# Wide tiles with rows of 2048 instead of 2112 bytes, and every pool 64 bytes further up

## The chip, the cores and the metric

The kernel runs on one core of a Trainium2 chip. TensorE (PE) multiplies matrices, VectorE (DVE) and ScalarE (ACT) work element by element, GpSimd (POOL) does small things and issues some of the transfers, SyncE (SP) issues the others. The engines run side by side and wait for each other by semaphores. Operands lie in SBUF, the core's own memory of 128 partitions; an address here is a byte within a partition, the same in all 128. TensorE writes its results to PSUM, in banks of 512 float32 per partition. A matmul has two operands in SBUF: the stationary one, 128 columns that are loaded ahead of it, and the moving one, here 256 or 512 columns of 4 bytes that stream through.

The metric is device time in microseconds, from runs of the whole program.

## The reference

One layer on a sequence of 512 tokens with 1024 features, all in float32. Three blocks follow each other, each with a norm ahead and behind and a residual:

```python
h = swiglu(rmsnorm(x, norm_ffn1_pre[l]), w_ffn1_in[l], w_ffn1_out[l])
x = x + FFN_RESIDUAL_SCALE * rmsnorm(h, norm_ffn1_post[l])
h = mixer(rmsnorm(x, norm_mix_pre[l]), w_mix_in[l], conv_w[l], conv_b[l],
          gate_i_bias[l], gate_f_bias[l], mlstm_norm[l], w_mix_out[l])
x = x + rmsnorm(h, norm_mix_post[l])
h = swiglu(rmsnorm(x, norm_ffn2_pre[l]), w_ffn2_in[l], w_ffn2_out[l])
x = x + FFN_RESIDUAL_SCALE * rmsnorm(h, norm_ffn2_post[l])
```

`swiglu` multiplies by a matrix of 1024 x 5632, gates one half with the other and multiplies by one of 2816 x 1024. The mixer projects to 3088 columns, runs a short convolution over one half and a two-way recurrent head (mLSTM, in chunks of 128) over the other, and projects back. The weights, some 86 MB by their shapes, come from HBM.

## The kernel before

**How products are made.** A float32 product is made of three matmuls in the type float32r: each operand is split into a high part (ScalarE copies it into float32r) and a low part (VectorE subtracts the copy), and high x high, high x low and low x high are added up in PSUM. `split` does this. On top of it, most of the large products use a seven-product scheme for 2 x 2 blocks in place of eight. So VectorE and ScalarE prepare weights all the time while TensorE multiplies.

**The stages**, in order of the program, with the line of the matmuls in each:

- Feed-forward, first matrix: `plain` (L542) for the first columns and `mm_part` (L516) for the rest, 256 moving columns each. The stationary operand is a block of weights, the moving one is the flipped activation, 4 rows of 128 features to a wide tile.
- Feed-forward, second matrix: `product_out` (L723) and `mm_out` (L745), with 512 moving columns. Here the moving operand is the weights and the stationary one a block of 128 columns of the activation.
- Mixer: L950 projects the values (256 and 272 moving columns in turn), `mm_cols` (L507) and `seven` with `mm_part` (L516) the rest; small matmuls for the heads (L1277 to L1370); L1425 projects back, 512 moving columns.
- The second feed-forward block, as the first.

TensorE's order is that of the program in most places; a scheduler orders the other engines' work when the program is built. That order is the same before and after the change on all engines.

**Where tiles lie.** Pools lie one behind the other in a partition: small constants, then `xpool` (4 tiles of 4096 bytes), `big` (13 wide tiles), `wpool` (12 of 4096: the split weights `whi`, `wlo`, `ws`, `wt`), `rawp` (4 of 4096: weights as loaded), then `gbp`, `t4p`, `t2p` (4096, 4096 and 2048 bytes). In the built program `xpool` starts at byte 7872, which is 30 x 256 + 192. All sizes behind it are multiples of 256, so every tile there starts at 192 more than a multiple of 256. This text calls what an address has over a multiple of 256 its remainder.

A wide tile is made by `bigt()`: 4 rows of `BW = 528` float32, 2112 bytes each, 8448 in all (33 x 256). Most users take the first 512 columns of a row; only a few need 528 (the mixer's values and their weights have 16 more columns for gates). Since 2112 is 8 x 256 + 64, the four rows start at remainders 192, 0, 64 and 128.

This sets the remainders of the operands:

| matmul line | moving operand | stationary operand |
|---|---|---|
| L542, L516, L507 | rows of wide tiles: 192, 0, 64, 128 in turn | weights in `wpool`: 192 |
| L723 | weights in `wpool`: 192 | blocks of a wide tile used as one row of 2048 columns, or of `xpool`: 192 |
| L745 | weights in `wpool`: 192 | rows of wide tiles: all four |
| L1425 | weights in `wpool`, or a wide tile used as one row: 192 | rows of wide tiles: all four |
| L950 | rows of 2112 bytes: all four | rows of wide tiles: all four |

The inner loop of L516, with `x` a view of a wide tile, shows how rows change with each matmul:

```python
for ww, xx in ((hi, 0), (hi, 1), (lo, 0)):
    for k in range(4):
        pin(nc.tensor.matmul(
            o, ww[:, k, :], x[xx][:, k, :], start=first and n == 0, stop=n == 11, skip_group_check=True))
```

Of the kernel before, what the change touches and what calls it, by code (L numbers as in the profile page):

```python
# [8 lines left out]
F32 = mybir.dt.float32  # L9
F32R = mybir.dt.float32r  # L10
# [6 lines left out]
P = 128  # L17
# [19 lines left out]
BW = 528  # L37
# [4 lines left out]
def encoder_kernel(ctx: ExitStack, tc: tile.TileContext, a: dict, out: bass.AP):  # L42
    nc = tc.nc

    const = ctx.enter_context(tc.tile_pool(name="const", bufs=1))
    xpool = ctx.enter_context(tc.tile_pool(name="xpool", bufs=NT))
    big = ctx.enter_context(tc.tile_pool(name="big", bufs=13))
# [11 lines left out]
    def nm(s):  # L59
        uid[0] += 1  # L60
        return f"{s}_{uid[0]}"

    def bigt(dt=F32):
        return big.tile([P, 4, BW], dt, tag="big", name=nm("big"))

    def ps():
        return psum.tile([P, 512], F32, tag="ps", name=nm("ps"))
# [10 lines left out]
    def f32(ap):  # L78
        return ap.bitcast(F32)

    def blk(i, n=P):
        return slice(i * n, (i + 1) * n)

    def ch(v):
        return v.rearrange("p (c t) -> p c t", t=P)
# [211 lines left out]
    def w_get(ahead=2):  # L297
        w_split(max(0, 1 + ahead - len(ready)))
        return ready.pop(0)
# [62 lines left out]
    def split(hi, lo, src, eng=nc.vector):  # L362
        latest["hi"] = nc.scalar.copy(out=hi, in_=src)  # L363
        if pinned["act"]:
            pin(latest["hi"])
        latest["lo"] = eng.tensor_tensor(out=lo, in0=src, in1=f32(hi), op=ALU.subtract)  # L366
        pin(latest["lo"])
# [34 lines left out]
    def xq_tile(xq, key):  # L402
        if key not in xq["q"]:
            xq["q"][key] = bigt(F32R)
        return xq["q"][key]
# [7 lines left out]
    def flip_q(tb, xs, xq, halves=(0, 1), bank=None):  # L413

        full = []
        for b in halves:
            pt = bank or ps()
            for k in range(4):
                pin(nc.tensor.transpose(out=pt[:, blk(k)], in_=xs[:, blk(4 * b + k)], identity=ident))  # L419
            hi, lo = xq_hl(xq, (b, tb // 2))  # L420
            split(hi[:, :, blk(tb % 2)], lo[:, :, blk(tb % 2)], ch(pt))
            if b not in xq["f"]:
                xq["f"][b] = bigt()
            if bank:
                return lambda fn: pin(fn(xq["f"][b][:, :, blk(tb)], ch(pt)))
            full.append((b, pt))
        for b, pt in full:
            pin(nc.scalar.copy(xq["f"][b][:, :, blk(tb)], ch(pt)))
# [91 lines left out]
    def ffn(xq, between, finish, mid=None, within=None, ahead=(2, 2, 1, 1), late=None, prep=None, block=0):  # L520
# [4 lines left out]


        h = [bigt() for _ in range((NF + 3) // 4)]
        spare.extend(h[-1][:, q, 0:512] for q in (2, 3))

# [362 lines left out]
    def v_split():  # L892
        for i in range(4):
            if not loaded:
                w_load(1)
            (raw,), _ = loaded.pop(0)
            bt = bigt(F32R).rearrange("p q f -> p (q f)")
            hi, lo = (bt[:, blk(n, 2 * BW)].rearrange("p (k f) -> p k f", k=2) for n in range(2))
            split(hi[:, :, 0:512], lo[:, :, 0:512], raw.rearrange("p (k f) -> p k f", k=2))
            rg = rawg[:, 2 * i:2 * i + 2, :]  # L900
            nc.gpsimd.tensor_copy(out=hi[:, :, 512:BW], in_=rg)
            nc.gpsimd.tensor_tensor(out=lo[:, :, 512:BW], in0=rg, in1=f32(hi[:, :, 512:BW]), op=ALU.subtract)
            wv.append((hi, lo))
# [14 lines left out]
    def within1(tb):  # L918
        if tb >= 2:
# [6 lines left out]
            (2, 1): lambda: flip_q(2, st1[2], xT1), (3, 0): lambda: mark.update(latest), (3, 1): lambda: flip_q(3, st1[3], xT1),  # L926
        },
        finish1, wgates, within1, (1, 1, 1, 0), late1, v_split)
    xq = st["xq"]

# [1 line left out]
        return xq_hl(xq, (k // 4, tb // 2))[hl][:, k % 4, blk(tb % 2)]  # L932


    vaug = bigt()
    vv = vaug.rearrange("p c (h e) -> p c h e", e=BW // 4)
    nc.gpsimd.memset(vv[:, :, :, DV:DV + 1], 1.0)
    spread = t2()
# [26 lines left out]
    with tc.issue_after(mark["pow"].ins):  # L965
        RA, RB = bigt(), bigt()
        nc.gpsimd.memset(RA[0:36, 0:2], 0.0)
        I, F = RA[0:36, 0, 0:512], RA[0:36, 1, 0:512]
        T1, T2 = RA[0:36, 2, 0:512], RA[0:36, 3, 0:512]
        B, A = RB[0:36, 0, 0:512], RB[0:36, 1, 0:512]  # L970
        CM, U = RB[0:36, 2, 0:512], RB[0:36, 3, 0:512]
        nc.gpsimd.memset(U, 1.0)
        nc.gpsimd.memset(ch(U)[:, :, 0:1], 0.0)
        HLT = bigt(F32R)
        UHL, IHL = HLT[:, 0, 0:512], HLT[:, 1, 0:512]
        nc.gpsimd.memset(f32(HLT[:, 0:2]), 0.0)
        sel = HLT.rearrange("p q f -> p (q f)")[:, 2 * BW:2 * BW + 8 * P].rearrange("p (j m) -> p j m", m=P)
        QT = bigt()
        Q1, Q2 = QT[:, 0, 0:512], QT[0:36, 1, 0:512]
        nc.gpsimd.memset(QT[:, 0:2], 0.0)  # L980
        parl = QT[0:36, 2, 0:2 * DK]
        nc.gpsimd.tensor_copy(parl.rearrange("p (e x) -> p e x", x=DK), par.broadcast_to([36, 2, DK]))
        gm = const.tile([36, 4, 8], F32, name="gm")
        amax, gsum, mprev, aco = gm[:, 0, 0:4], gm[:, 1, 0:4], gm[:, 2, :], gm[:, 3, 0:4]
        nc.vector.memset(mprev[:, 0:1], NEG)
# [261 lines left out]
        pn2[:, 256:272], parl, acd.rearrange("p q c -> p (q c)"),  # L1247
        start=True, stop=True,
    )
    Ct = bigt()  # L1250
    Cf = Ct.rearrange("p q f -> p (q f)")
    Cs = Cf[:, 0:12 * 129].rearrange("p (q i e) -> p q i e", q=4, i=3)
    nat1 = Cf[:, 1552:2064].rearrange("p (c r) -> p c r", r=P)
# [147 lines left out]
    for n, k in enumerate(MIXK):  # L1401
        if n < 5:
            wmo[k] = w_get(0)
        else:
            raw = rawp.tile([P, 1024], F32, tag="raw", name=nm("raw"))
            nc.sync.dma_start(raw, wo[blk(k), :])
            bt = bigt(F32R).rearrange("p q f -> p (q f)")
            split(bt[:, 0:1024], bt[:, 1024:2048], raw)
            wmo[k] = (bt[:, 0:1024], bt[:, 1024:2048])
    for tb in range(NT):  # L1410
# [58 lines left out]
```

## Time and profile before

| | |
|---|---|
| median of 3 runs | 888.0 us (886.79 to 888.97) |
| the profiled execution | 888.25 us, span from first to last instruction 886.5 us |
| mean granted TensorE clock | 0.999 |
| TensorE busy | 99% of the span, 6039 matmuls |
| VectorE, ScalarE, GpSimd busy | 83%, 55%, 11% |
| DMA | 123.24 MB, 139 GB/s on average |

The page of a profile gives busy times of the engines, a picture of the span in slices, the DMA queues, the chain of work that ended last (followed back from the last instruction, step by step, to what released it), and the costliest groups of instructions. A group's row has the line, engine, operation, what is written and read (`ps<-big,whi`: the moving operand first, then the stationary one), the shape and the count; then busy time, the mean duration of one, and the idle time ahead of it with what ended it. The chain can also be had in order of time: start, length, and how many instructions of one line followed each other. Matmul durations are modelled and overlap, so a matmul's real cost is read from start to start.

### The profile page before, as it was taken

How to read it: one execution, taken by the hardware profiler on the slowest of the kernel's cores; microseconds unless marked ns; L12 is line 12 of the kernel's file. 1: busy time of each engine (PE TensorE's matmuls, PEld its weight loads, DVE VectorE, ACT ScalarE, POOL GpSimd, SP SyncE). 2: the span in 40 equal slices, each digit the busy share in tenths (PEclk: the TensorE clock that was granted, in tenths of full speed). 3: DMA queues.
4: the chain of work that ended last, by engine and by line, in shares of the span. 5: the costliest groups of instructions: out<-in, count | busy, mean ns of one | idle time of the engine just before them, and what ended most of it. 6: DMA issues, size and time to landing. Idle time of an engine off the chain costs nothing.

```text
span 886.5 us, 15403 instructions
## 1 busy us (share of the span) xinstructions
PE 875.6 (99%) x6039; PEld 807.4 (91%) x6039; DVE 731.8 (83%) x1159; ACT 491.8 (55%) x855; POOL 93.7 (11%) x123
## 2 busy tenths in 40 slices
PE   8999999999999999999999999999999999999997
PEld 6999999999988889988988888999999999988885
DVE  6989898988889978887588757898898988869956
ACT  7656455544656645755565535654555555546722
POOL 5000000001132022100121011000000000223000
PEclk9999999999999999999999999999999999999999
DMA  8444433424998852442062733433333423899722
GB/s 255 126 120 121 118 94 98 118 84 129 216 261 201 278 181 83 121 118 71 1 190 91 213 111 102 128 105 108 96 96 96 132 83 105 201 243 231 267 72 95
DMA packets 140384, 123.24 MB, mean 139 GB/s; under 512 B 5500, under 2 KB 116112, under 8 KB 140312
## 3 DMA queue, kind: packets, MB, share of 16 engines
q1 hardware_dynamic: 129936, 97.62, 36.8%
q0 software_dynamic: 10368, 24.65, 12.5%
q8 instruction: 47, 0.77, 0.3%
q14 instruction: 25, 0.20, 0.1%
q10 hardware_dynamic: 8, 0.01, 0.0%
HBM read 115.96 MB, written 6.29 MB: 138 GB/s over the span
## 4 chain that ended last, share of the span: by engine, by line
PE 96%; DMA 1%; DVE 1%; issue 0%; ACT 0%; DVEq 0%; POOLq 0%; POOL 0%; ACTq 0%
PE ps L516 47%; PE ps L723 19%; PE ps L507 9%; PE ps L542 5%; PE ps L1425 5%; PE ps L745 5%; PE ps L950 3%; DMA raw<-in_w_mix_in_dram 1%; PE ps L419 1%; PE ps L1328 1%; DMA g_row<-in_norm_ffn_pre_dram 1%; PE ps L472 0%; PE ps L1336 0%; PE ps L1277 0%; DVE t L464 0%
## 5 line engine op out<-in xcount | busy, mean ns | idle before, releaser
L516 PE MATMUL ps<-big,whi 128*128 128x256 f32 x2064 | 283.8, 280 | 0.4 <-DVE t L1086 0.4
L516 PEld LDWEIGHTS ps<-big,whi 128*128 128x128 f32 x2064 | 261.0, 188 | 1.9 <-DVE t L1086 0.8
L363 ACT CAST whi<-raw 128x1024 fp32r<-128x1024 f32 x170 | 175.5, 1051 | 72.6 <-DVE raw L216 23.6
L366 DVE TENSOR_TENSOR wlo<-raw,whi 128x1024 fp32r<-128x1024 f32 x166 | 201.3, 1220 | 13.0 <-ACT whi L363 8.7
L516 PE MATMUL ps<-big,wlo 128*128 128x256 f32 x1032 | 161.6, 280 | 0.0
L516 PEld LDWEIGHTS ps<-big,wlo 128*128 128x128 f32 x1032 | 138.8, 188 | 0.0
L723 PE MATMUL ps<-whi,big 128*128 128x512 f32 x336 | 105.7, 389 | 0.0
L723 PEld LDWEIGHTS ps<-whi,big 128*128 128x128 f32 x336 | 62.9, 188 | 13.0
L516 PE MATMUL ps<-big,ws 128*128 128x256 f32 x516 | 69.9, 280 | 0.0
L170 POOL DMA_DIRECT2D raw<-in_w_ffn_out_dram x18 | 22.0, 1221 | 440.6 <-DMA raw<-in_w_ffn_out_dram 222.5
L723 PE MATMUL ps<-wlo,big 128*128 128x512 f32 x168 | 64.8, 389 | 0.0
L516 PEld LDWEIGHTS ps<-big,ws 128*128 128x128 f32 x516 | 64.7, 188 | 0.0
L690 ACT COPY t<-ps 128x256 f32<-128x256 f32 x40 | 14.9, 373 | 88.4 <-PE ps L516 88.4
L507 PE MATMUL ps<-big,whi 128*128 128x512 f32 x224 | 55.2, 397 | 0.0
L507 PEld LDWEIGHTS ps<-big,whi 128*128 128x128 f32 x224 | 41.4, 188 | 9.3
L363 ACT CAST whi<-t 128x1024 fp32r<-128x1024 f32 (+1 forms) x44 | 39.5, 913 | 15.3 <-DVE t L216 10.2
L366 DVE TENSOR_TENSOR wlo<-t,whi 128x1024 fp32r<-128x1024 f32 (+1 forms) x44 | 46.2, 1051 | 1.4 <-ACT whi L363 0.7
L745 PE MATMUL ps<-whi,big 128*128 128x512 f32 x128 | 40.3, 393 | 0.0
L723 PEld LDWEIGHTS ps<-wlo,big 128*128 128x128 f32 x168 | 31.5, 188 | 6.5
L692 DVE TENSOR_TENSOR t<-ps,t 128x256 f32<-128x256 f32 x40 | 16.9, 423 | 20.7 <-PE ps L516 20.5
L542 PE MATMUL ps<-big,whi 128*128 128x256 f32 x256 | 33.8, 283 | 0.0
L542 PEld LDWEIGHTS ps<-big,whi 128*128 128x128 f32 x256 | 31.7, 188 | 0.6 <-ACT big L363 0.3
(245 smaller groups left out, 1408.0 us busy)
## 6 DMA issues: line engine op xcount, KB each, us to landing
raw<-in_w_ffn_in_dram SPq DMA_DIRECT2D x68, 512.0 KB, 4.6
raw<-in_w_ffn_out_dram SPq DMA_DIRECT2D x26, 512.0 KB, 4.7
raw<-in_w_mix_in_dram SPq DMA_DIRECT2D x24, 512.0 KB, 4.7
t<-in_w_ffn_in_dram SPq DMA_DIRECT2D x20, 512.0 KB, 3.7
raw<-in_w_ffn_out_dram SPq DMA_DIRECT2D x36, 256.0 KB, 6.2
raw<-in_w_ffn_out_dram POOLq DMA_DIRECT2D x18, 512.0 KB, 7.8
xd<-x POOLq DMA_DIRECT2D x8, 512.0 KB, 2.9
x<-xd POOLq DMA_DIRECT2D x8, 512.0 KB, 5.2
```

The source lines that it names most:

```text
L170: nc.gpsimd.dma_start(sums.rearrange("p (g f) -> p g f", g=2), top[:, 512:1024].rearrange("p (g f) -> p g f", g=1).broadcast_to([P, 2, 512 ...
L363: latest["hi"] = nc.scalar.copy(out=hi, in_=src)
L366: latest["lo"] = eng.tensor_tensor(out=lo, in0=src, in1=f32(hi), op=ALU.subtract)
L507: nc.tensor.matmul(o, w[ww][:, k, :], xq_tile(xq, (k // 4, xx))[:, k % 4, FULL], start=n == 0, stop=n == 3 * KD - 1)
L516: pin(nc.tensor.matmul(o, ww[:, k, :], x[xx][:, k, :], start=first and n == 0, stop=n == 11, skip_group_check=True))
L542: pin(nc.tensor.matmul(o, ww[:, k, :], xq_hl(xq, (k // 4, th))[xx][:, k % 4, :], start=n == 0, stop=n == 3 * KD - 1))
L690: nc.scalar.copy(a_[:, h1], x[:, h0])
L692: nc.vector.tensor_tensor(out=c[:, h1], in0=y[:, h0], in1=a_[:, h1], op=ALU.add)
L723: nc.tensor.matmul(acc[tb + t][half], left[n][x][:, blk(t)], right[n][y], start=first and x == y == 0, stop=last_ and x == 1, skip_group_c ...
L745: nc.tensor.matmul(acc[tb][half], hT[hh][:, blk(tb)], w[ww][:, blk(half, 512)], start=fresh and hh == ww == 0, stop=k == NF - 1 and hh == ...
L950: nc.tensor.matmul(pv_[i][:, 0:at.stop - at.start], xv(xx, k, tb), ww[:, k % 2, at], start=n == 0, stop=n == 3 * KD - 1)
L1425: nc.tensor.matmul(acc[half], yy[yi][:, k % 4, blk(tb)], wmo[k][wi][:, blk(half, 512)], start=(n == 0 and yi == 0 and wi == 0), stop=(n == ...
```

## The change

`wide()` now makes the tile as one row of 2112 float32, and `bigt()` gives the first 2048 columns of it as four rows of 512: 2048 bytes from row to row. The tile keeps its 8448 bytes. Those who need 528 columns (the weights of the values in `v_split`, `vaug`, `Ct`) or the tile as one long row (`v_split`, the last three blocks of the mixer's output weights) take `wide()`. `sel` moves from column 1056 to column 1024 of its tile, the third row as before. A constant tile of 64 bytes that nothing uses, `room`, moves everything behind it up by 64: `xpool` starts at 7936 = 31 x 256, so that every tile behind it has remainder 0, and every row that `bigt()` gives as well. Only rows of 2112 bytes (`vaug` and the weights in `v_split`, the moving operand of L950) still lie at all four remainders.

Instructions, their order and their waits stay the same on all engines; three memsets of two rows each become 1024 instead of 1056 columns.

```diff
+    def wide(dt=F32):
+        return big.tile([P, 4 * BW], dt, tag="big", name=nm("big"))
+
     def bigt(dt=F32):
-        return big.tile([P, 4, BW], dt, tag="big", name=nm("big"))
+        return wide(dt)[:, 0:2048].rearrange("p (q f) -> p q f", q=4)
+
+    const.tile([P, 16], F32, name="room")
...
-            bt = bigt(F32R).rearrange("p q f -> p (q f)")
+            bt = wide(F32R)
             hi, lo = (bt[:, blk(n, 2 * BW)].rearrange("p (k f) -> p k f", k=2) for n in range(2))
...
-    vaug = bigt()
+    vaug = wide().rearrange("p (q f) -> p q f", q=4)
...
-        sel = HLT.rearrange("p q f -> p (q f)")[:, 2 * BW:2 * BW + 8 * P].rearrange("p (j m) -> p j m", m=P)
+        sel = HLT.rearrange("p q f -> p (q f)")[:, 8 * P:16 * P].rearrange("p (j m) -> p j m", m=P)
...
-    Ct = bigt()
+    Ct = wide().rearrange("p (q f) -> p q f", q=4)
...
-            bt = bigt(F32R).rearrange("p q f -> p (q f)")
+            bt = wide(F32R)
             split(bt[:, 0:1024], bt[:, 1024:2048], raw)
```

## The prediction

> **What bounds the kernel now.** I read the page first: the busy times, then the chain that ended last. The sequence of instructions is the same before and after on every engine, so what can change is how long an instruction takes where it stands; the next views are therefore those that give a time for each matmul.
>
> ```profile
> PE 875.6 (99%) x6039; PEld 807.4 (91%) x6039; DVE 731.8 (83%) x1159; ACT 491.8 (55%) x855; POOL 93.7 (11%) x123
> PE 96%; DMA 1%; DVE 1%; issue 0%; ACT 0%; DVEq 0%; POOLq 0%; POOL 0%; ACTq 0%
> PE ps L516 47%; PE ps L723 19%; PE ps L507 9%; PE ps L542 5%; PE ps L1425 5%; PE ps L745 5%; PE ps L950 3%; DMA raw<-in_w_mix_in_dram 1%; PE ps L419 1%; PE ps L1328 1%; DMA g_row<-in_norm_ffn_pre_dram 1%; PE ps L472 0%; PE ps L1336 0%; PE ps L1277 0%; DVE t L464 0%
> ```
>
> 96% of the chain is TensorE, and seven matmul lines hold 93% of it. TensorE hardly waits, so the kernel's time is the number of matmuls times the time from one start to the next. I call that time the pitch. The durations in the groups (280 or 389 ns) are modelled and overlap; the pitch comes from the chain view, where an unbroken run of one line stands as start, length and count:
>
> ```profile
> 24.03 13.38 PE ps L542 x112
> 37.41 196.29 PE ps L516 x1668
> 233.70 2.76 PE ps L723 x12
> 237.87 83.00 PE ps L723 x366
> 344.80 8.75 PE ps L950 x72
> 376.67 27.34 PE ps L507 x118
> 504.14 22.27 PE ps L1425 x96
> 779.21 78.92 PE ps L723 x348
> 858.13 22.09 PE ps L745 x96
> ```
>
> Length over count: 117.7 ns at L516, with 256 columns. With 512 columns: 226.8 at L723 (both long runs), but 231.7 at L507, 230.1 at L745 and 232.0 at L1425. L723 has the same shape as these three:
>
> ```profile
> L516 PE MATMUL ps<-big,whi 128*128 128x256 f32 x2064 | 283.8, 280 | 0.4 <-DVE t L1086 0.4
> L516 PE MATMUL ps<-big,wlo 128*128 128x256 f32 x1032 | 161.6, 280 | 0.0
> L723 PE MATMUL ps<-whi,big 128*128 128x512 f32 x336 | 105.7, 389 | 0.0
> L516 PE MATMUL ps<-big,ws 128*128 128x256 f32 x516 | 69.9, 280 | 0.0
> L507 PE MATMUL ps<-big,whi 128*128 128x512 f32 x224 | 55.2, 397 | 0.0
> L542 PE MATMUL ps<-big,whi 128*128 128x256 f32 x256 | 33.8, 283 | 0.0
> L507 PE MATMUL ps<-big,wlo 128*128 128x512 f32 x112 | 28.2, 394 | 0.0
> L542 PE MATMUL ps<-big,wlo 128*128 128x256 f32 x128 | 18.0, 282 | 0.0
> L353 PE MATMUL ps<-rawg 128*128 128x256 bf16 x6 | 0.8, 272 | 0.0
> 9.60 0.82 PE L353 MATMUL ps<-rawg 128*128 128x256 bf16 x6
> ```
>
> What separates them in the code is where operands lie. Before, narrow tiles and a wide tile's first row start at 192 more than a multiple of 256; the other rows of a wide tile at 0, 64 and 128. At L723 both operands always start at 192. At L507, L516 and L542 the moving operand (named first) goes through the four rows of a wide tile in turn, so its remainder changes with each matmul; at L745 and L1425 the stationary one does. So the trace holds 512-wide matmuls with equal remainders and with changing ones: equal is 3.3 to 5.2 ns shorter. It holds no long run of 256-wide ones with equal remainders.
>
> L353 shows how short a 256-wide pitch can be: six bf16 matmuls in 0.82 us, the last one 272 ns long, so (820 - 272) / 5 = 110 ns. Against that L516 loses 8 ns.
>
> **The change part by part.** After it, all rows that these lines read start at remainder 0, except the moving rows of L950, which keep 2112 bytes.
>
> *512-wide lines with wide rows.* L507 has 336 matmuls (224 and 112 above), L745 and L1425 have 192 each. I take the pitch of L723, 226.8, for them: nothing but remainders is meant to differ, and that both lie at 0 instead of 192 should not matter where they are equal. L507: 336 x 4.9 = 1.6 us; L745: 192 x 3.3 = 0.6; L1425: 192 x 5.2 = 1.0. Sum -3.3 us, all on the path. Ends: -3.3, and nothing if the difference has another cause (below).
>
> *L723*, 756 matmuls, 19% of the chain: equal before and after, 0.
>
> *256-wide lines.* L516 has 2064 + 1032 + 516 = 3612 and L542 has 256 + 128 = 384, together 3996. This term decides, and no row shows it. Two bounds from the nearest rows: if changing remainders cost a fixed 4.9 ns for each matmul (231.7 - 226.8), the new pitch is 112.8; if they cost nothing at this width, it stays 117.7. Between: L507 less L516 is 231.7 - 117.7 = 114.0 ns for 256 more columns, so what is left for a matmul as such is 117.7 - 114.0 = 3.7, and the rest grows with the columns. With 3.7 kept, the 226.8 of L723 makes (226.8 - 3.7) / 2 + 3.7 = 115.25 for half the width. I take that: 3996 x 2.45 = -9.8 us. Ends: 3996 x 4.9 = -19.6 and 0.
>
> *L950*: 121.5 ns for 256 and 272 columns in turn; one operand's rows still change. 0.
>
> *VectorE and ScalarE* read and write wide rows too. Same form, one with a wide row and one without:
>
> ```profile
> L366 DVE TENSOR_TENSOR ws<-t,ws 128x512 fp32r<-128x512 f32 x43 | 29.4, 685 | 0.2 <-ACT ws L363 0.2
> L366 DVE TENSOR_TENSOR wlo<-big,whi 128x512 fp32r<-128x512 f32 x22 | 15.1, 688 | 2.9 <-ACT whi L363 2.9
> L967 POOL MEMSET big<- 36x1056 f32 x1 | 1.0, 972 | 0.0
> 37.00:234.00 197.00, 197.00 (x1674) 196.92 (x1673) 173.51 (x275) 104.59 (x171) 5.01 (x4) 1.00 0.42 117
> ```
>
> 685 and 688 ns: no difference to win. Three memsets on GpSimd shrink by 3% of 1 us, off the chain: 0. The last row is the first L516 stretch: of 197 us TensorE is busy throughout, VectorE 173.5, ScalarE 104.6. A pitch of 115.25 shortens it by 4 us, so VectorE, the next to be late, has room left (173.5 in 193), and the gain is not given back there.
>
> *DMA landings.* Every destination moves from remainder 192 to 0. Where loads are in the chain:
>
> ```profile
> 2.18 4.84 DMA g_row<-in_norm_ffn_pre_dram
> 446.68 8.34 DMA raw<-in_w_mix_in_dram
> t<-in_w_ffn_in_dram SPq DMA_DIRECT2D x20, 512.0 KB, 3.7
> raw<-in_w_mix_in_dram SPq DMA_DIRECT2D x24, 512.0 KB, 4.7
> ```
>
> The first is 8 KB, all latency. The second ends with one 512 KB load; the fastest class of that size lands in 3.7 us against 4.7, so at best -1.0 us. I take 0: no row shows a landing at another remainder. Elsewhere transfers lie under TensorE, busy all the time. DMA: Bandwidth & Descriptors of the Trainium skill, section How a descriptor splits into AXI transactions, says that a transaction must start at a multiple of 256 bytes; for 512 bytes from 192 that makes 22 beats of 32 bytes instead of 16. If it held for writes into SBUF, an estimate from that page would be a quarter off the transfer part of these landings; no row here can show it.
>
> Sum: -3.3 - 9.8 = -13.1 us. The profiled execution took 888.25 us (span 886.5), 0.25 above the median of 888.0. 888.25 - 13.1 = 875.
>
> **Rivals.**
>
> *Only the 512-wide lines gain.* 256-wide matmuls may be held by something that does not care about remainders: at L950 remainders differ by 0 or 128 only, and its 121.5 ns over 264 columns on average is no better than L516's 117.7 over 256 with 4 ns for the 8 columns. Then -3.3: 885.
>
> *No change at all.* The 4.9 ns between L507 and L723 could come from the order of products: L723 moves to another accumulator after three matmuls, L507 after 24. Against it: L745 takes 12 in a row and lies at 230.1, L1425 takes 24 and lies at 232.0, so the pitch does not follow that count well. Then 888. SBUF — State Buffer of the Trainium skill, section Who interferes with whom, says that TensorE and ScalarE never wait on anyone at the SBUF; by that rule the pitch depends on shape alone and the change gives nothing. The rows 226.8 and 231.7 of one shape speak against it.
>
> *Slower: a beat.* L723 needs a while to reach 226.8: its short run of 12 lies at 230.0. It looks as if a stream with equal remainders settles into a fixed rhythm, which then may only be a whole number of beats, while changing remainders let the pitch lie between two of them, as 117.7 does. 226.8 is 17 beats of 13.33 ns. If that is the beat, 256 columns need 9 of them, 120.0 (8 would be 106.7, under the 110 of L353). Price: 3996 x 2.3 = +9.2, less 3.3: 894. With half the beat, 17 x 6.67 = 113.3 is allowed, and it would be -17.6 - 3.3: 867. It decides against the change where the 256-wide pitch passes 117.7 + 3.3 / 3.996 = 118.5. No row shows a beat directly.
>
> *Much faster.* Remainder 0 takes away the whole loss, also at L723: 256-wide 110 as L353, 512-wide twice that, 220. 3996 x 7.7 = 30.8 us, L507 336 x 11.7 = 3.9, L745 192 x 10.1 = 1.9, L1425 192 x 12.0 = 2.3, L723 756 x 6.8 = 5.1: together 44, so 844. Against it: L950 has both operands at 0 for some of its matmuls and its mean is no better; and the first L516 stretch would shrink by 13 us to 184, with VectorE's 173.5 nearly filling it.
>
> **How the numbers follow.** Main case, both widths gain, 0.45; its own range is 867 (113.3 ns) to 881 (116.9 ns). Only 512-wide: 0.17. No change: 0.12. Slower by the beat: 0.16. Much faster: 0.10. This kernel's times tell 0.3%, 2.7 us, from no change. Faster: 0.45 + 0.10 + 0.10 (of the 3.3 us of the second case, as it is only just over 2.7) = 0.65; same: 0.07 + 0.12 = 0.19; slower 0.16. The range runs from 862, below the pitch of 113.3, to 892, which takes in no change and the lesser part of the beat; it leaves out the great gain and the full price of the beat.
>
> **What would show it.** Right: L507, L745 and L1425 at 227 ns in the chain view, L723 still 226.8, L516 between 113 and 117 and VectorE busier as a share. Wrong: L516 at 117.7 (the second rival) or at 120 (the beat), L507 still at 231.7 (remainders are not the cause), L723 itself below 226 (remainder 0 is special and not only equal remainders). If L516 falls but the span doesn't, idle time in front of TensorE would have appeared, for VectorE first.

## The result and the profile after

The kernel became slower. Five runs took 893.11 to 894.43 us, median 893.49; the ratio to the kernel before is 1.0068, with a 95% interval of 1.0056 to 1.0079, so the loss of about 6 us is real. The profiled execution took 893.49 us with a span of 891.5, 5.0 more than the span before.

The change makes the kernel five lines longer at the `bigt` helper, which moves the line numbers: L516 of before is L521 now, L542 is L547, L507 is L512, L723 is L728, L745 is L750, L1425 is L1430 and L950 is L955. First the busy line and the chain's shares from the page of the kernel after, then its chain in order of time (start, length, line and how many matmuls followed each other):

```profile
PE 882.8 (99%) x6039; PEld 817.0 (92%) x6039; DVE 730.8 (82%) x1159; ACT 492.2 (55%) x855; POOL 94.8 (11%) x123
PE 96%; DVE 1%; DMA 1%; SPq 1%; issue 0%; ACT 0%; DVEq 0%; POOLq 0%; POOL 0%; ACTq 0%
```

```profile
37.26 200.16 PE ps L521 x1668
...
241.60 82.99 PE ps L728 x366
...
348.16 8.76 PE ps L955 x72
...
380.02 26.78 PE ps L512 x118
...
506.04 21.79 PE ps L1430 x96
...
577.63 197.28 PE ps L521 x1644
...
863.54 21.77 PE ps L750 x96
```

TensorE is 96% of the chain as before, so the difference must lie in the pitch, and it does, with both signs. The 512-wide lines gained: L512 has 226.9 ns (26.78 / 118) instead of 231.7, L1430 227.0 instead of 232.0, L750 226.8 instead of 230.1. L728 is unchanged at 226.8, and so is L955 at 121.7. But L521, with 256 columns, has 120.0 ns in both long stretches (200.16 / 1668 and 197.28 / 1644), where it had 117.7: 3.9 us lost in the first and 3.8 in the second. All 3996 matmuls of this width at 2.3 ns make +9.2 us, the 512-wide lines give back about 3.2, and that leaves +6.0; the spans differ by 5.0, the medians by 5.5. From start to start L521 goes at 120, 120, 120 ns, while L516 of before went at 117, 118, 119, 116, 117, 118, 115, 120: with equal remainders the rhythm is fixed.

The other engines did not move. In the groups by shape of the kernel after, VectorE needs 682 and 684 ns for the two forms that took 685 and 688, and in the first long stretch TensorE is busy throughout, beside 172.6 us of VectorE (173.5 before):

```profile
L371 DVE TENSOR_TENSOR ws<-t,ws 128x512 fp32r<-128x512 f32 x43 | 29.3, 682 | 0.4 <-ACT ws L368 0.4
37.26:237.42 200.16, 200.16 (x1670) 200.16 (x1669) 172.56 (x274) 104.08 (x170) 5.01 (x4) 1.00 0.41 115
raw<-in_w_mix_in_dram SPq DMA_DIRECT2D x24, 512.0 KB, 4.6
t<-in_w_ffn_in_dram SPq DMA_DIRECT2D x20, 512.0 KB, 3.6
```

The last two rows are DMA issues of the kernel after: 4.6 and 3.6 us to landing, where it was 4.7 and 3.7.

### The profile page after: what moved, and what is told of

Read it like the earlier page. It is cut to its first block, busy times and chain, and to the rows that moved or that the text cites. A ratio compares the mean times of both kernels' runs of the same rounds, so it can differ in the third digit from the quotient of the medians.

```text
span 891.5 us, 15403 instructions
## 1 busy us (share of the span) xinstructions
PE 882.8 (99%) x6039; PEld 817.0 (92%) x6039; DVE 730.8 (82%) x1159; ACT 492.2 (55%) x855; POOL 94.8 (11%) x123
## 4 chain that ended last, share of the span: by engine, by line
PE 96%; DVE 1%; DMA 1%; SPq 1%; issue 0%; ACT 0%; DVEq 0%; POOLq 0%; POOL 0%; ACTq 0%
PE ps L521 49%; PE ps L728 19%; PE ps L512 9%; PE ps L1430 5%; PE ps L750 5%; PE ps L547 4%; PE ps L955 3%; DMA x<-in_x_dram 1%; PE ps L1333 1%; PE ps L1341 0%; SPq L318 0%; PE ps L424 0%; PE ps L477 0%; PE ps L1282 0%; PE ps L1309 0%
## 5 line engine op out<-in xcount | busy, mean ns | idle before, releaser
L521 PE MATMUL ps<-big,whi 128*128 128x256 f32 x2064 | 288.6, 283 | 0.0
L521 PEld LDWEIGHTS ps<-big,whi 128*128 128x128 f32 x2064 | 266.2, 192 | 1.2 <-ACT t L1314 0.2
L521 PE MATMUL ps<-big,wlo 128*128 128x256 f32 x1032 | 164.2, 283 | 0.0
L521 PEld LDWEIGHTS ps<-big,wlo 128*128 128x128 f32 x1032 | 141.7, 192 | 0.0
L728 PE MATMUL ps<-whi,big 128*128 128x512 f32 x336 | 105.6, 389 | 0.0
L728 PEld LDWEIGHTS ps<-whi,big 128*128 128x128 f32 x336 | 63.0, 188 | 13.0
L521 PE MATMUL ps<-big,ws 128*128 128x256 f32 x516 | 71.2, 283 | 0.0
L521 PEld LDWEIGHTS ps<-big,ws 128*128 128x128 f32 x516 | 66.0, 192 | 0.0
L728 PE MATMUL ps<-wlo,big 128*128 128x512 f32 x168 | 64.7, 389 | 0.0
L512 PE MATMUL ps<-big,whi 128*128 128x512 f32 x224 | 54.5, 394 | 0.0
L512 PEld LDWEIGHTS ps<-big,whi 128*128 128x128 f32 x224 | 41.4, 188 | 8.7
L750 PE MATMUL ps<-whi,big 128*128 128x512 f32 x128 | 39.8, 390 | 0.0
L728 PEld LDWEIGHTS ps<-wlo,big 128*128 128x128 f32 x168 | 31.6, 188 | 6.4
L547 PE MATMUL ps<-big,whi 128*128 128x256 f32 x256 | 34.5, 285 | 0.2 <-DVE big L371 0.2
L547 PEld LDWEIGHTS ps<-big,whi 128*128 128x128 f32 x256 | 32.2, 191 | 0.9 <-DVE big L371 0.4
```

Of the source, the lines that this page charges most:

```text
L512: nc.tensor.matmul(o, w[ww][:, k, :], xq_tile(xq, (k // 4, xx))[:, k % 4, FULL], start=n == 0, stop=n == 3 * KD - 1)
L521: pin(nc.tensor.matmul(o, ww[:, k, :], x[xx][:, k, :], start=first and n == 0, stop=n == 11, skip_group_check=True))
L547: pin(nc.tensor.matmul(o, ww[:, k, :], xq_hl(xq, (k // 4, th))[xx][:, k % 4, :], start=n == 0, stop=n == 3 * KD - 1))
L728: nc.tensor.matmul(acc[tb + t][half], left[n][x][:, blk(t)], right[n][y], start=first and x == y == 0, stop=last_ and x == 1, skip_group_c ...
L750: nc.tensor.matmul(acc[tb][half], hT[hh][:, blk(tb)], w[ww][:, blk(half, 512)], start=fresh and hh == ww == 0, stop=k == NF - 1 and hh == ...
```

## The experiments

The theory after this result was the rival of the beat: with operands at equal remainders the pitch settles at a whole number of steps of one beat, which for 256 columns makes 120.0. Against it stood three others: that remainder 0 is a bad place as such, that moving the pools does it, or that the pitch follows from the direction in which the rows step over the remainders.

### Rows alone, pools alone

The first takes `room` out of the kernel after, so that all rows lie at equal remainders of 192; the second puts only `room` into the kernel before.

```diff
-    const.tile([P, 16], F32, name="room")
```

> Rows of 2048 bytes, pools where they were: every row that the large products read starts at remainder 192 instead of 0. Beat theory: a matmul can only start on a grid of 6.67 ns, and the grid moves with the remainder of its moving operand; what slows the 256-wide ones is that all remainders are equal, not that they are 0. So as the changed kernel: the 256-wide pitch 120.0 ns, the 512-wide lines 226.8, time 893 to 894. Rival, multiples of 256 collide: the fault is remainder 0; at 192 the 256-wide pitch is 117.7 or less and the 512-wide lines keep their gain: 885 or less.

```diff
+    const.tile([P, 16], F32, name="room")
```

> Rows of 2112 bytes as before, pools 64 bytes further up: the stationary weights start at remainder 0 and the moving rows at 0, 64, 128, 192 in turn. Beat theory: the steps between remainders are those of before, so 888 and 117.7 ns. Rival, multiples of 256 collide: three quarters of the way to nothing, one quarter of the 256-wide matmuls meets 0 with 0: 889 to 890; and if transfers that land at remainder 0 bring anything, 887.

The rows alone: 893.35 us, ratio 1.0066 (1.0051 to 1.0081), the whole loss. The pools alone: 887.36, ratio 0.9998 (0.9989 to 1.0008), nothing. From the chain in order of time, first of the rows alone, then of the pools alone:

```profile
36.62 200.16 PE ps L521 x1668
...
379.36 26.78 PE ps L512 x118
```

```profile
37.12 196.41 PE ps L518 x1668
...
376.50 27.34 PE ps L509 x118
```

At remainder 192 L521 has the same 120.0 ns and L512 the same 226.9 as at 0; with the pools moved and the rows at 2112 bytes, L518 has 117.8 and L509 231.7, as before. What counts so far is whether the rows lie at one remainder or at four, not at which.

### The rows taken in reverse

The kernel before, with the four moving rows of L516 and L542 taken from the last to the first.

```diff
-            for k in range(4):
+            for k in (3, 2, 1, 0):
...
-                for k in range(KD):
+                for k in (3, 2, 1, 0, 7, 6, 5, 4):
```

> The kernel before, with the four rows of a wide tile taken in the order 3, 2, 1, 0 at the 256-wide lines, so that the moving operand's remainder goes down by 64 from matmul to matmul instead of up. Same instructions, sums in another order. Beat theory: the grid of 6.67 ns shifts the other way, by +1.67 ns a matmul instead of -1.67, so that 17 steps and a shift are 115.0 ns instead of 18 steps less a shift, 118.3, or 18 steps, 120.0: 3996 x 2.65 = 10.6 us less, 877. Rival, any change of remainder is as good as any other (two streams that meet by chance): 117.7 ns and 888.

890.39 us, ratio 1.0032 (1.0022 to 1.0041). In its chain, the first long stretch:

```profile
36.42 197.41 PE ps L516 x1668
```

118.4 ns, 0.7 worse than forwards, and not the 115.0 that a law of shifts would give. 3996 matmuls at 0.7 ns make the 2.6 us that it lost. The order of the rows matters a little; that law falls.

### Matmuls alone

A program of matmuls only, which leaves out all else that the reference computes: stretches of 96 or 72, each with its own width and places. `mov` and `st` are float32r tiles; 16 columns are 64 bytes, so the first stretch (its matmuls are L42) keeps both at one remainder and the second (L46) moves the moving operand by 64 bytes from matmul to matmul.

```diff
+    # 256 moving +0
+    for n in range(96):
+        m, s = 0 * (n % 4) + 512 * (n % 3), 128 * (n % 8)
+        keep(mm(bank(n, 256), st[:, s:s + 128], mov[:, m:m + 256], **flags(n)))
+    # 256 moving +64
+    for n in range(96):
+        m, s = 16 * (n % 4) + 512 * (n % 3), 128 * (n % 8)
+        keep(mm(bank(n, 256), st[:, s:s + 128], mov[:, m:m + 256], **flags(n)))
```

> A kernel of its own that computes nothing of the reference: runs of 72 to 96 matmuls in float32r with nothing else going on, one source line for each run, that differ in the columns, in how the remainder of the moving or the stationary operand goes from matmul to matmul, and in how far apart the two are. Beat theory: 256 columns, moving operand +0: 120.0 ns; +64: about 117.7; +128: 116.7 (17.5 steps); +192, which is -64: 115.0. 512 columns: 226.7, 231.7, 230.0, 228.3. A constant distance between stationary and moving makes no difference to equal remainders. Equal remainders with 192 to 496 columns: only multiples of 6.67 ns. Rival, the collision of two equal remainders: 256 columns with a constant distance of 64 to 192 is faster than 120.0, and the direction of the step makes no difference; the pitch grows smoothly with the columns.

From its chain in order of time: the 256-wide moving operand stepping by 64 (L46), 512 columns at equal remainders (L58) and stepping by 64 (L62), the stationary operand held 64 bytes off (L98), both operands at 64 (L126), then widths at equal remainders: 232 columns (L146), 320 (L170), 384 (L174), 448 (L178):

```profile
21.04 11.36 PE bank L46 x96
...
55.16 21.79 PE bank L58 x96
76.94 22.25 PE bank L62 x96
...
244.42 11.31 PE bank L98 x96
...
356.49 11.51 PE bank L126 x96
...
403.61 8.04 PE bank L146 x72
...
455.16 10.55 PE bank L170 x72
465.71 12.48 PE bank L174 x72
478.19 14.88 PE bank L178 x72
```

With nothing else running, the pitches of the kernels are there again. 256 columns: 118.3 stepping, 119.9 at equal remainders (120.0 between the starts once a stretch has settled, at remainders 0, 32 and 64 alike). 512 columns: 226.7 at equal remainders between the starts, 231.7 stepping by 64. So no other engine, no wait and no DMA makes the difference between equal and changing remainders. Stepping backwards gives 118.4 here, the same as forwards; why the kernel before has 117.7, which is 0.6 less, stays open.

The widths speak for the beat only in part. Between starts, 320 columns take 146.7 ns, 384 take 173.3, 448 take 206.7 and 512 take 226.7: 22, 26, 31 and 34 steps of 6.67 ns, and 120.0 is 18. If there is a step, it is half of what the rival had taken, for 31 is odd. But 256, 320, 384 and 512 columns also lie on one straight line, 26.7 ns for 64 columns and 13.3 for the matmul as such, and 26.7 is four steps, so their whole numbers follow from the line alone. Only 448 columns, 6.7 above it, speak for a step. Two more things did not fit the expectation. Widths that are no multiple of 64 columns lie between steps (248 columns 115.0, 264 columns 120.1, 272 columns 125.3), so the step is not a clock that every matmul waits for. And from 192 to 232 columns the pitch stays at 111.7; what holds it there was not measured.

With a step of 6.67 ns, 17 steps (113.3) are allowed for 256 columns as well. The stretch with the stationary operand 64 bytes off, at 117.8, showed that constant remainders need not mean 18 steps, nor any whole number of them.

### Weights 64 bytes off

The kernel after, with 64 bytes between `big` and `wpool`: wide tiles at 0, weights at 64.

```diff
+    shift = ctx.enter_context(tc.tile_pool(name="shift", bufs=1))
     wpool = ctx.enter_context(tc.tile_pool(name="wpool", bufs=12))
...
+    shift.tile([P, 16], F32, name="apart")
```

> The changed kernel with 64 bytes more between the wide tiles and the split weights: all remainders still constant, but weights at 64 and wide tiles at 0. Meeting theory (the load of the next stationary operand and the moving stream, at the same remainder, fall into one rhythm of whole steps): the 256-wide pitch is what the probe gave for a distance of 64, 117.8 instead of 120.0, 3996 x 2.2 = 8.8 us less; the 512-wide lines leave their 226.8 for the probe's 228.9 (weights moving, L728, L750, L1430, 1140 of them) and 233.3 (weights stationary, L512, 336): 2.4 + 2.2 us more. Together 893.5 - 8.8 + 4.6 = 889. Rival, constancy alone (any operand that starts at the same remainder each time falls into whole steps): 120.0 stays, 893 to 894.

877.14 us, with runs of 872.63, 873.43, 880.86 and 880.85; ratio 0.9884 (0.9842 to 0.9926). It is faster than both kernels, where 117.8 ns had been expected. In the chain of the profiled execution (872.63):

```profile
36.11 189.04 PE ps L523 x1668
...
229.28 83.77 PE ps L730 x366
...
368.75 27.53 PE ps L514 x118
...
495.52 22.15 PE ps L1432 x96
...
566.80 186.32 PE ps L523 x1644
```

L523 has 113.33 ns in both stretches: 17 steps. The 512-wide lines pay for it, since their operands are 64 apart now too: 228.9 at L730, 233.3 at L514, 230.7 at L1432. The times come in two groups, whose means are 7.8 us apart; 1668 x (117.8 - 113.3) is 7.5 us, about what one long stretch at the other pitch would cost. No execution of the slower group was traced here; one of the next kernel was.

### More places, alone

The second program of matmuls goes through 16 distances between the operands, 16 bytes apart, and several places of the rows; it too computes nothing of the reference.

```diff
+    for n in range(60):  # L53
+        m, s = 0 * (n % 4) + 512 * (n % 3), 16 + 128 * (n % 8)
+        keep(mm(bank(n, 256), st[:, s:s + 128], mov[:, m:m + 256], **flags(n)))  # 256: rows 0 on, apart 64
```

> Matmuls alone again, nothing of the reference: 256 columns with the moving operand's four rows 0, 16, 32, 48 or 64 bytes further in turn and the stationary operand 0 to 240 bytes apart in steps of 16, 60 matmuls each; and 512 columns with constant remainders, 0 to 240 apart. Meeting theory: with rows 0 on, 120.0 at 0 apart and 117.8 at 64 and 192; some arrangement may lie clearly below 117.7, towards the 111.7 that loading alone takes. Rival, constancy: all of the row at 0 on lies at 120.0 or 113.3. For 512 columns the least is at 0 apart, 226.7, by the first; no difference by the second.

In its chain, distances of 48 and 64 bytes:

```profile
30.21 7.07 PE bank L50 x60
37.28 6.81 PE bank L53 x60
```

Between starts it is 117.7 and 113.3. With the moving operand's remainder held, 64 bytes is the one distance of the 16 with the short pitch (the others have 116.7 to 120.1), and the first program had 117.8 for the same distance. With 512 columns, distances of 0, 16 and 240 bytes have 226.7, and all others cost 2 to 8 ns more. So a distance that is good for one width is not good for the other: 512 columns want the operands together, and 256 gain most at 64.

### Apart for one width, together for the other

Built on the kernel with the weights 64 bytes off: wide tiles that serve as stationary or as one row start 64 bytes in, so that L731, L753 and L1433 have equal remainders, while the moving rows of L524 and L550 stay 64 bytes from the weights.

```diff
-    def bigt(dt=F32):
-        return wide(dt)[:, 0:2048].rearrange("p (q f) -> p q f", q=4)
+    def bigt(dt=F32, at=0):
+        return wide(dt)[:, at:at + 2048].rearrange("p (q f) -> p q f", q=4)
...
-    const.tile([P, 16], F32, name="room")
-    shift.tile([P, 16], F32, name="apart")
+    shift.tile([P, 48], F32, name="ahead")
+    apart.tile([P, 16], F32, name="apart")
...
-                    hs = bigt(F32R)
+                    hs = bigt(F32R, 16)
```

> From the kernel with 64 bytes between wide tiles and weights: the wide tiles that serve as stationary operands (L731, L753, L1433) start 64 bytes further inside their tile, so that 512-wide matmuls of these lines have both operands at one remainder again, while the 256-wide ones (L524, L550) and L515 keep their 64 bytes. Meeting theory: L524 at 113.3 ns (or 117.8, the probe and the chip have shown both at that distance), L731, L753 and L1433 at 226.7, L515 at 233.3: 756 x 2.1 + 192 x 2.1 + 192 x 3.7 = 2.7 us less than that kernel, 870 in executions that lie at 113.3, 878 where a long stretch of L524 lies at 117.8. Rival, constancy: 120.0 ns for L524 and 893.

877.99 us, from 870.03 to 879.27 in two groups; ratio 0.9862 (0.9827 to 0.9897). In the chain of one execution (879.27):

```profile
38.31 196.45 PE ps L524 x1668
...
238.91 82.96 PE ps L731 x366
...
574.41 186.32 PE ps L524 x1644
...
849.25 21.77 PE ps L753 x96
```

The 512-wide lines are back at 226.7 and 226.8. L524 shows both pitches in one execution, at the same places: 117.8 in the first stretch and 113.3 in the second. So at a distance of 64 the pitch is not set by the places alone. Whether it is how the stretch begins, the next program tries.

### Which distance holds by itself

The third program starts each place three times, each start after twelve matmuls of another width, and goes through distances of the stationary operand from 0 to 252 in steps of 4 bytes. It computes nothing of the reference.

```diff
+    for r in range(3):
+        disturb(r)
+        for n in range(48):
+            m, s = 512 * (n % 3), 16 + 128 * (n % 8)
+            keep(mm(bank(n, 256), st[:, s:s + 128], mov[:, m:m + 256], **flags(n)))  # apart 64
```

> Matmuls alone, nothing of the reference: 256 columns, constant remainders, the stationary operand 0 to 252 bytes apart in steps of 4; three runs of 48 for each distance, with twelve matmuls of 128, 168 or 208 columns ahead of them so that they start at different moments. Meeting theory: at 0 apart 120.0 whatever went ahead; near 64 apart two rhythms, 113.3 and 117.8, and which of them is held depends on the moment of the start. If one distance holds 113.3 in all three, it is the better place. Rival, that 113.3 was an accident of one place in memory: it does not come back, 117.8 everywhere near 64.

In its chain, all three starts at distance 64 (L130), and the first and last at distance 76 (L145):

```profile
357.69 5.50 PE bank L130 x48
...
364.50 5.69 PE bank L130 x48
...
371.51 5.67 PE bank L130 x48
```

```profile
420.59 5.50 PE bank L145 x48
...
434.24 5.49 PE bank L145 x48
```

Each length includes the change from the matmuls ahead; once settled it is, from start to start, 113.3, 117.8 and 117.8 at 64, and 113.3 all three times at 76, as at 88. At distance 0 it is 120.0 to 120.1 in all three. Only what went ahead differs between the three starts, so at 64 the start does decide, which fits the two groups of the kernels.

### Distances 76 and 88 in the kernel

The kernel before with rows of 2048 bytes and all pools at 192; the moving tiles start 180 or 168 bytes in, which puts the stationary operand 76 or 88 ahead of them.

```diff
-            xq["q"][key] = bigt(F32R)
+            xq["q"][key] = bigt(F32R, 45)
```

> Rows of 2048 bytes and pools where they were, so that everything lies at remainder 192; only the wide tiles that are moving operands of the 256-wide matmuls start 45 columns (180 bytes) further inside, so that the stationary weights are 76 bytes ahead of them. In the probe this distance held 113.3 ns in three runs of three. Meeting theory: L519 and L545 at 113.3 in every execution, L726, L748 and L1428 at 226.7, L510 at about 232: 3996 x 4.3 + 0.7 + 0.9 = 18.8 us less than before, 869, and no second group of times at 877. Rival, that the probe's distances do not carry over (the rhythm depends on which tiles in SBUF the streams come from): L519 at 117 to 120 and 885 to 893.

```diff
-            xq["q"][key] = bigt(F32R)
+            xq["q"][key] = bigt(F32R, 42)
```

> The same with 42 columns (168 bytes), a distance of 88 bytes, the other one that held 113.3 ns in three probe runs of three. Meeting theory: 869 as well, in every execution. Rival: as for 76 bytes; and if 76 and 88 differ here though the probe had them equal, its distances carry over only in part.

Both missed: 897.86 us, ratio 1.014 (1.0116 to 1.0165), and 896.48, ratio 1.0106 (1.0093 to 1.0119). From the chains, of 76 first:

```profile
37.63 200.16 PE ps L519 x1668
...
380.57 28.20 PE ps L510 x118
```

```profile
36.88 200.16 PE ps L519 x1668
...
379.72 28.12 PE ps L510 x118
```

120.0 ns in both, and 239.0 and 238.3 for 512 columns. At 76 the six runs went from 897.20 to 904.13 us, again not in one group; the profiled one took 898.23. The program had shifted the stationary operand with the moving one at 0, the kernel the moving one with the stationary fixed. Either the distance alone doesn't decide, or the program says nothing about the kernel.

### The moving operand shifted, alone

To tell these two apart, the fourth program (again nothing of the reference) keeps the stationary operand and shifts the moving one by 0 to 252 bytes, with five starts each.

```diff
+    for r in range(5):
+        disturb(r)
+        for n in range(48):
+            m, s = 28 + 512 * (n % 3), 128 * (n % 8)
+            keep(mm(bank(n, 256), st[:, s:s + 128], mov[:, m:m + 256], **flags(n)))  # moving at 112
```

> Matmuls alone, nothing of the reference: 256 columns, the stationary operand always at remainder 0, as the weights can be had in the kernel, and the moving one at 0 to 252 in steps of 4; five runs of 48 for each, started at different moments. Meeting theory with the distance alone: moving at 180 and 168 (stationary 76 and 88 ahead) hold 113.3, as in the probe before, and what the kernels at 76 and 88 showed, 120.0, came from their other work. Rival, the moving operand's own place within 64 bytes counts too (in the probe before it was always 0): 180 and 168 give 120.0 here as well; 192 (64 ahead) 113.3 or 117.8. If some place holds 113.3 in all five, it is one to try in the kernel.

From its chain, one of the five starts each of the moving operand at 112 bytes (L190) and at 168 (L260):

```profile
1010.01 5.56 PE bank L190 x48
```

```profile
1503.72 5.81 PE bank L260 x48
```

At 168 it is 120.0 and at 180 it is 120 or 123 between starts, depending on the start. The traced kernels have 120.0 at both, so the program does carry over, and the distance alone does not decide; the second value at 180 would fit the spread of the kernel at 76. At 112 it settles at 113.3 in five starts of five, and at 192 either 113.3 or 117.8 (the two pitches of the kernels with a distance of 64).

### The moving rows 112 bytes on

The same kernel with the moving tiles 112 bytes past the remainder of the weights.

```diff
-            xq["q"][key] = bigt(F32R)
+            xq["q"][key] = bigt(F32R, 28)
```

> As the kernels at 76 and 88, with the moving wide tiles of the 256-wide matmuls 28 columns (112 bytes) inside their tile, so that they start 112 bytes past the weights' remainder. This place held 113.3 ns in five probe runs of five, and the probe gave the 120 of the kernels at 76 and 88 when the moving operand lay as it does there. Both operands' places count: L519 and L545 at 113.3 in every execution, L726, L748 and L1428 at 226.7, L510 at 233: 3996 x 4.3 + 0.7 + 0.9 - 0.5 = 18.3 us less than before, 869 to 870, without the second group of times at 878. Rival, the rhythm that a long run holds depends on what goes on beside it: L519 at 117 to 120 and 880 to 893.

869.17 us, from 868.65 to 870.23 in one group; ratio 0.9793 (0.9779 to 0.9806), as expected. The chain in order of time, and the first long stretch with the busy time of each engine:

```profile
36.56 189.04 PE ps L519 x1668
...
229.74 82.99 PE ps L726 x366
...
368.06 27.28 PE ps L510 x118
...
493.88 21.79 PE ps L1428 x96
...
564.21 186.32 PE ps L519 x1644
...
839.14 21.77 PE ps L748 x96
```

```profile
36.56:225.60 189.04, 189.04 (x1669) 189.04 (x1669) 172.67 (x274) 103.85 (x171) 5.01 (x4) 1.00 0.45 123
```

L519 has 113.33 ns in both stretches, L726, L1428 and L748 keep 226.8 to 227.0, and L510, whose moving rows are these same tiles, has 231.2. This version is 2.1% faster than the kernel before and, by the medians, 2.7% faster than the kernel after. It is the changed rows of 2048 bytes with another start.

## Why the prediction was wrong, point by point

**What bounds the kernel** was right: only the pitch of the matmuls changed, in both directions, and it moved the span. Matmuls alone showed the same pitches.

**The 512-wide lines** were right, by size too: -3.3 us forecast from L723's 226.8, and L507, L745 and L1425 came out at 226.8 to 227.0. That remainder 0 is as good as 192 where operands are equal was assumed; L723 (226.8 at both) and the kernel with the rows alone showed it.

**The 256-wide lines** are the step that failed. The prediction took "(226.8 - 3.7) / 2 + 3.7 = 115.25 for half the width", -9.8 us; it measured 120.0, +9.2 us. The slope behind it, 114.0 ns for 256 more columns, came from rows with changing remainders. With equal ones 256 more columns take 226.7 - 120.0 = 106.7, so that 13.3 ns are left for a matmul as such where the prediction kept 3.7; the 146.7 and 173.3 of 320 and 384 columns, measured alone, lie on the same line. A slope from operands that lie one way was carried over to operands that lie another. The bounds failed with it: both ends, "a fixed 4.9 ns" and "nothing", let equal remainders help or do nothing, and no row excluded that they hurt. This term is off by 19.0 us; forecast and result differ by 18.5.

**The beat** was the rival that gave the right numbers. It named 120.0 ns and 894 us, and the point from which it decides, 118.5. What spoke for it stood in the prediction: L723 takes a while to reach its 226.8, and that streams with equal remainders settle into a fixed rhythm is shown. Its reason for 120.0 is not, and that it named the right pitch is in part luck: it took nine beats of 13.33, while the 206.7 of 448 columns and the 113.3 are no whole number of such beats. With a beat of 6.67 it lacked a reason for 120.0 over 113.3, which it named as the other way. Both exist: equal remainders hold 120.0, the moving rows 112 bytes on hold 113.3, and a distance of 64 takes 113.3 or stays at 117.8, which is no whole number of either beat. No row of before could have told which.

**The other rivals.** "Only the 512-wide lines gain" and "no change at all" fell with L521 and L512. L950 did not move, 121.5 to 121.7, as said. "Much faster", with remainder 0 taking away the whole loss, fell: 0 and 192 gave the same pitches. The first two of these rested on remainders not mattering, for one width or for both; matmuls alone show 226.7 to 234.4 ns for one shape. SBUF — State Buffer of the Trainium skill, section Who interferes with whom, by which TensorE waits on nobody, doesn't hold here if it is read as a pitch that depends on the shape alone. The measurement decides.

**VectorE and ScalarE** at 0 were right (682 ns against 685). The cover that the prediction named was not tried by this change, since TensorE got slower, but it was by the last version: with the stretch at 189.0 us VectorE's 172.7 still fit under TensorE, which was busy throughout.

**DMA landings** at 0 were right for the time. The mixer's load, from which the prediction allowed at best -1.0 us, is not in the chain after; TensorE was busy for 19.59 of the 20 us around it before (440 to 460 us), so little could be won there. The two classes shown went from 4.7 to 4.6 and from 3.7 to 3.6 us. Seven executions with their destinations at remainder 192 (the kernel before and six of the experiments) have 4.5 to 4.7 and 3.7 to 4.0; the two at 0 (the kernel after and the pools alone) have 4.6 and 3.6 both times. So the first class gains nothing, and the second a tenth at most. A quarter off the transfer part, which the estimate from DMA: Bandwidth & Descriptors of the Trainium skill, section How a descriptor splits into AXI transactions, would give, is not seen; how much of a landing is transfer was not measured.

**What stays open.** Shown is that the pitch follows the places of both operands, that equal remainders hold 120.0 and 226.7, and that the lost time of the change is this. Why the places do it was not measured: that the reads of the two operands meet in the memory, as the expectations have it, is a theory. Whether there is a step of 6.67 ns at all is open too. Where the pitch depends on the start, what in the start decides was not tried either.

## What to carry to other kernels

In a kernel that TensorE bounds, read the pitch of each matmul shape from long runs in the chain, length over count, and compare equal shapes: differences of 2 to 6% with no wait in the profile can come from where operands lie. Aligned rows are not better as such, and the two widths here had different good places, so measure a few starts of the moving against the stationary operand with matmuls alone, both placed as in the kernel, and don't work out the pitch of one width from another whose operands lie otherwise. Start each place several times, since a place whose pitch depends on the start makes times in two groups.

## What the runs showed of the hardware

All for float32r with 128 stationary columns, at a granted clock of 0.995 or more:

| what | ns from start to start |
|---|---|
| 256 columns, equal remainders (0, 32, 64 or 192) | 120.0 |
| 256 columns, rows of 2112 bytes in turn | 117.7; reversed 118.4 |
| 256 columns, moving operand 112 bytes past the stationary one | 113.3 |
| 256 columns, stationary operand 64 bytes past the moving one | 113.3 or 117.8 |
| 512 columns, equal remainders | 226.7 |
| 512 columns, moving operand 180 bytes past the stationary one | 239.0 |
| 192 to 232 columns, equal remainders | 111.7 |

By the last row, going from 232 columns down to 192 brought nothing; each of these matmuls loads its weights anew.
